# A diffusion layer on one core: splits off GpSimd, joined block transfers, keys over GpSimd's queue, unread products at the routing

## The chip, the core and the metric

The kernel runs on one of the eight cores of a Trainium2 chip. A core has five engines with queues of their own: TensorE (PE in the profile: matrix products into PSUM), VectorE (DVE), ScalarE (ACT), GpSimd (POOL) and SyncE (SP), which mostly issues DMA transfers; ScalarE and GpSimd issue some too. Each engine works through its instructions in order, and semaphores tie them together. The metric is device microseconds of one execution, the median of three runs.

## What is computed

One layer of a hybrid backbone over 1024 latent and 256 context tokens of width 1024: one input projection (2832 columns), softmax attention (8 query heads on 2 key heads of 64), a gated delta rule (4 heads of 128, both directions), one output projection, then 16 experts that each choose 128 tokens. The reference, cut:

```python
p_lat = h_lat @ w_in                      # split into aq ak av dq dk dv dz db da
...
att_lat = merge_heads(attend_blocked(q_l, k_all, v_all))   # softmax over context and latent keys
...
qkv = jax.nn.silu(short_conv(jnp.concatenate([dq, dk, dv], axis=-1), conv_w))
...
decay = jnp.exp(jnp.where(tril, g_cum[..., :, None] - g_cum[..., None, :], -jnp.inf))
a_strict = jnp.where(tril & ~eye, jnp.einsum('bhnid,bhnjd->bhnij', k_beta, k) * decay, 0.0)
unit_lower = a_strict + eye.astype(f32)
sol = lax.linalg.triangular_solve(unit_lower, rhs, left_side=True, lower=True, unit_diagonal=True)
...
def step(s, inp):                          # scan over chunks, once per direction
    v_new = u_c - jnp.einsum('bhck,bhkv->bhcv', w_c, s)
    s_next = s * gl_c[..., None, None] + jnp.einsum('bhck,bhcv->bhkv', kd_c, v_new)
    o = jnp.einsum('bhck,bhkv->bhcv', qd_c, s) + jnp.einsum('bhij,bhjv->bhiv', qk_c, v_new)
...
y_lat = jnp.concatenate([att_lat, dn_lat], axis=-1) @ w_out
x = x + g1 * y_lat
affinity = jax.nn.softmax((h @ router_w).astype(jnp.float32), axis=-1)
gates, idx = lax.top_k(jnp.swapaxes(affinity, 1, 2), cap)
hid = jax.nn.silu(xg @ w_gate) * (xg @ w_up)     # by expert
x = x + g2 * scatter_add((hid @ w_down) * gates)
```

## The kernel before, in words

The kernel is written in Python; a scheduler sets each engine's order of instructions at build time. Tokens go in 10 tiles of 128 (two of context, eight latent). float32 products are made from split operands, a high part (`whi`, `hh`, `ehi`) and a rest (`wlo`, `hl`, `elo`), three products for each.

**Stages** (us from the span's start): modulation and hidden tokens to 72; input projection to 411; attention groups with the scan steps of the delta rule to about 715; attention with the output projection and the routing to 978; experts to 1526; the last stores.

**Projection** (`in_proj`). The columns come in groups: keys and values of attention, then k, q, v of the delta rule (`conv_head`, `conv_tail`), attention queries (`queries`), the gate z (`out_gate`). `weights` loads each group's next weights (`wraw`), rounds them on ScalarE (`whi`, L425) and forms the rest `wlo` (L426), from the seventh group on GpSimd and earlier on VectorE. Between the groups `tick` draws steps from a generator (`prep`): the decay gates; `dn_chunk` for each of the ten chunks; the inverses (`dn_wave`); the rotary tables and the rotation of the attention keys (`sr_raw`, `sr_b`, `sr_sp`, stored in DRAM as `sks` and `sqs`).

`dn_chunk` loads k and q of one chunk, head-transposed (`kq`, L803 and L805, two transfers), and the cumulated decay spread over all partitions (`grow`, L807). GpSimd subtracts the token's own decay (L808), ScalarE makes Relu and exp of it (L814, L815: `Ef`, `Eb`, for latent chunks also `Eq`). TensorE multiplies k with k and q (L825, L827, into PSUM banks `ps_d`), VectorE multiplies the banks with the decays (L829, L830, L834), GpSimd masks (`affine_select`, L843), and SP stores `sN` and `sQ`. `kq`, `grow` and the decays have two buffers each.

`dn_wave` inverts the 32x32 diagonal blocks of 8 units at once (a unit is a chunk and a direction) by VectorE steps on `T` (L864, L866), in three waves; ScalarE makes a transposed copy (L869) and stores both in DRAM (`sT`, L870, L871). Wave 0 runs in the projection, the others beside the scans.

**Scans.** After `att_open` (which loads the rotated keys, `ksplit`, L1052, and transposes them, L1056) and `dn_open` (zeroed blocks `F` and `X`), each of ten rounds runs a `dn_step` in both directions and an attention group (`att_group`). A `dn_step` loads k, v, q, `kT` and the blocks of `sT` (`dn_merge`: eight transfers of 16 KB, L896, and `mN`, L898), merges the blocks to the inverse of 128x128 by small products (L907 to L942), and updates the state `S` (L975 to L1009). Attention goes by query blocks j (two tiles of tokens) and four head pairs hp: scores (L1112), transposes of the probabilities (L1122), values. `att_q(j)` prepares the block's transposed queries `QT` (L1080); it is called at hp = 2 of the block before, and for j = 0 at the first group.

**Routing.** Each expert's tokens are found by sorted lists that VectorE merges (`top_in`, `top_out`; L1402 spreads a list, L237 merges), then their minimum is spread (L1452), ranks are counted, the tokens of experts 0 and 1 picked (L1500) and gathered by GpSimd, and transposed (L1526). Then the experts' products begin (L1601).

The lines that the change moves, as they stand:

```python
(eng or nc.vector).tensor_tensor(lo[:, k:k + 4], raw, hi[:, k:k + 4], op=ALU.subtract)
...
nc.sync.dma_start(kq[:, :, 0], self.skT[c])
if lat:
    nc.sync.dma_start(kq[:, :, 1], self.sqT[c])
...
nc.gpsimd.tensor_tensor(gr, gr, self.gc[:, c, :, None].to_broadcast([P, 8, P]), op=ALU.subtract)
...
nc.sync.dma_start(s, self.sks[t0:t0 + T].rearrange("t p i d -> p t i d"))
...
if hp == 2 and j < 3:
    self.att_q(j + 1)
```

## Time and profile before

| | |
|---|---|
| median of 3 runs | 1551.98 us (1550.82 to 1552.12) |
| profiled execution | 1550.66 us |
| its span | 1548.9 us, mean granted clock 0.967 |
| PE busy | 1443.1 us (93%) |
| DVE busy | 1178.0 us (76%) |
| ACT busy | 949.0 us (61%) |
| POOL busy | 222.8 us (14%) |

Times in the rows count from the span's start. A busy PE row is not PE at its peak, since products overlap. A line of a view by stretches gives the stretch and its length, then the busy time with the number of instructions for PE, PEld (weight loads), DVE, ACT and POOL, then PE's granted clock (1.00 is full), the share of DMA and GB/s. A line of the waits names the engine and line that waited, the engine and line that it waited for, the total in us, the number of times and the longest. A line of the groups gives line, engine, operation, tiles, shapes and count, busy us and mean ns, then idle time before. In the timeline: start, duration, engine and line; in brackets the idle time before and what ended it. SPq is SP's DMA queue.

### The profile page before, as it was taken

How to read it: one execution, taken by the hardware profiler on the slowest of the kernel's cores; microseconds unless marked ns; L12 is line 12 of the kernel's file. 1: busy time of each engine (PE TensorE's matmuls, PEld its weight loads, DVE VectorE, ACT ScalarE, POOL GpSimd, SP SyncE). 2: the span in 40 equal slices, each digit the busy share in tenths (PEclk: the TensorE clock that was granted, in tenths of full speed). 3: DMA queues.
4: the chain of work that ended last, by engine and by line, in shares of the span. 5: the costliest groups of instructions: out<-in, count | busy, mean ns of one | idle time of the engine just before them, and what ended most of it. 6: DMA issues, size and time to landing. Idle time of an engine off the chain costs nothing.

```text
span 1548.9 us, 25613 instructions
## 1 busy us (share of the span) xinstructions
PE 1443.1 (93%) x9416; PEld 1173.8 (76%) x9416; DVE 1178.0 (76%) x2456; ACT 949.0 (61%) x1513; POOL 222.8 (14%) x230
## 2 busy tenths in 40 slices
PE   4899998997899999999899996799999999999997
PEld 1887787886777787788577664688888888888885
DVE  2825578698678686576574588899999999999996
ACT  2815455434285544566774543688888888888884
POOL 0000003423111121111400021111111111111101
PEclk7999999997999999999999998899999999999999
DMA  9356826777734456541342575889999999999992
GB/s 356 103 187 212 287 84 180 223 237 247 224 82 146 138 176 183 143 136 53 94 149 94 181 292 211 315 300 394 382 396 394 394 387 391 399 396 384 381 371 43
DMA packets 187048, 377.27 MB, mean 244 GB/s; under 512 B 47631, under 2 KB 124187, under 8 KB 159403
## 3 DMA queue, kind: packets, MB, share of 16 engines
q1 hardware_dynamic: 176320, 339.94, 61.9%
q0 software_dynamic: 7488, 29.36, 6.3%
q10 hardware_dynamic: 3115, 6.34, 1.1%
q8 instruction: 74, 1.21, 0.3%
q14 instruction: 51, 0.42, 0.1%
HBM read 321.91 MB, written 53.68 MB: 242 GB/s over the span
## 4 chain that ended last, share of the span: by engine, by line
PE 71%; DVE 12%; DMA 8%; ACT 5%; issue 2%; POOL 1%; SPq 1%; POOLq 0%; ACTq 0%; DVEq 0%
PE ps_m L1601 32%; PE ps_t L1129 4%; PE ps_a L1112 3%; PE ps_t L1122 3%; PE ps_s L441 3%; PE ps_s L443 3%; PE ps_s L442 3%; PE ps_t L1601 2%; PE ps_d L975 1%; DMA woraw<-in_w_out 1%; DMA sz<-zz 1%; PE ps_d L296 1%; PE ps_d L981 1%; PE ps_d L1284 1%; PE ps_d L1283 1%
## 5 line engine op out<-in xcount | busy, mean ns | idle before, releaser
L1601 PE MATMUL ps_m<-ehi,xx 128*128 128x512 f32 x1024 | 259.7, 396 | 0.4 <-DVE xx L1538 0.4
L1601 DVE TENSOR_TENSOR elo<-eraw,ehi 128x2048 fp32r<-128x2048 f32 x102 | 231.3, 2288 | 20.1 <-ACT ehi L1601 19.6
L1601 ACT ACTIVATE ehi<-eraw 128x2048 fp32r<-128x2048 f32 x105 | 201.3, 1918 | 54.7 <-PE ps_m L1601 45.4
L1601 PEld LDWEIGHTS ps_m<-ehi,xx 128*128 128x128 f32 x1024 | 189.9, 189 | 38.3 <-ACT xf L1534 0.8
L1601 PE MATMUL ps_m<-elo,xx 128*128 128x512 f32 x512 | 137.4, 390 | 0.0
L1601 PE MATMUL ps_m<-ehi,hx 128*128 128x512 f32 x512 | 129.7, 395 | 0.0
L1115 DVE TENSOR_SCALAR_CACHE_REDUCE prob<-ps_a 128x416 f32<-128x416 f32 (+1 forms) x192 | 109.4, 595 | 26.0 <-PE ps_a L1112 16.2
L1601 DVE TENSOR_TENSOR elo<-fraw,ehi 128x2048 fp32r<-128x2048 f32 x51 | 115.8, 2287 | 9.1 <-ACT ehi L1601 9.0
L1112 PE MATMUL ps_a<-kts,QT 128*128 128x416 f32 (+1 forms) x384 | 109.1, 390 | 4.0 <-DVE prob L1115 3.9
L1601 ACT ACTIVATE ehi<-fraw 128x2048 fp32r<-128x2048 f32 x51 | 97.8, 1917 | 24.2 <-PE ps_m L1601 21.4
L1601 PEld LDWEIGHTS ps_m<-elo,xx 128*128 128x128 f32 x512 | 96.3, 188 | 20.5
L1123 ACT ACTIVATE PT<-ps_t 128x512 f32<-128x512 f32 (+1 forms) x192 | 93.7, 525 | 28.8 <-PE ps_t L1122 26.9
L1601 PEld LDWEIGHTS ps_m<-ehi,hx 128*128 128x128 f32 x512 | 94.0, 188 | 18.2
L1122 PE MATMUL ps_t<-consts,prob 128*128 128x128 f32 x640 | 100.2, 282 | 3.1 <-ACT PT L1123 1.7
L433 PE MATMUL ps_s<-whi,hh 128*128 128x256 f32 (+1 forms) x336 | 98.0, 293 | 3.9 <-DVE zz L625 2.1
L1745 POOL DMA_INDIRECT out_x<-ey,idx x16 | 52.0, 3252 | 342.3 <-DVE ey L1601 342.3
L1118 ACT ACTIVATE prob<-prob,mn 128x1280 f32<-128x1280 f32 x64 | 87.2, 1363 | 19.1 <-DVE mn L1117 18.4
L435 PE MATMUL ps_s<-whi,hl 128*128 128x256 f32 (+1 forms) x336 | 95.8, 289 | 0.9 <-DVE hl L410 0.9
L434 PE MATMUL ps_s<-wlo,hh 128*128 128x256 f32 (+1 forms) x336 | 95.5, 287 | 0.0
L441 PE MATMUL ps_s<-hh,whi 128*128 128x512 f32 (+1 forms) x256 | 95.1, 372 | 0.0
L443 PE MATMUL ps_s<-hh,wlo 128*128 128x512 f32 (+1 forms) x256 | 94.3, 368 | 0.0
L442 PE MATMUL ps_s<-hl,whi 128*128 128x512 f32 (+1 forms) x256 | 94.0, 367 | 0.0
(434 smaller groups left out, 3134.5 us busy)
## 6 DMA issues: line engine op xcount, KB each, us to landing
eraw<-in_w_up SPq DMA_DIRECT2D x38, 1024.0 KB, 9.4
eraw<-in_w_down SPq DMA_DIRECT2D x32, 1024.0 KB, 7.0
eraw<-in_w_gate SPq DMA_DIRECT2D x31, 1024.0 KB, 8.8
wmod<-in_w_mod SPq DMA_DIRECT2D x24, 1024.0 KB, 6.3
fraw<-in_w_down SPq DMA_DIRECT2D x21, 1024.0 KB, 7.6
fraw<-in_w_gate SPq DMA_DIRECT2D x16, 1024.0 KB, 9.8
fqraw<-in_w_gate SPq DMA_DIRECT2D x16, 1024.0 KB, 9.7
fraw<-in_w_up SPq DMA_DIRECT2D x14, 1024.0 KB, 8.4
```

Source lines behind the costliest of these rows:

```text
L433: self.nc.tensor.matmul(ps[:, :n], self.hh[:, k, ts], hi[:, k, a:a + n], start=st, stop=False)
L434: self.nc.tensor.matmul(ps[:, :n], self.hh[:, k, ts], lo[:, k, a:a + n], start=False, stop=False)
L435: self.nc.tensor.matmul(ps[:, :n], self.hl[:, k, ts], hi[:, k, a:a + n], start=False, stop=en)
L441: self.nc.tensor.matmul(ps[:, :n], hi[:, k, a:a + P], self.hh[:, k, ts], start=st, stop=False)
L442: self.nc.tensor.matmul(ps[:, :n], hi[:, k, a:a + P], self.hl[:, k, ts], start=False, stop=False)
L443: self.nc.tensor.matmul(ps[:, :n], lo[:, k, a:a + P], self.hh[:, k, ts], start=False, stop=en)
L1112: nc.tensor.matmul(ps[:, k0:min(k0 + 512, w)], QT[:, h, i], self.KTs[:, kv * 2 + x, ks], start=x == 0, stop=x == 1)
L1115: v.tensor_scalar(pr[:, c0:c0 + w], ps[:, :w], -1.0, 3e38, op0=ALU.mult, op1=ALU.min, accum_out=mn[:, y:y + 1])
L1118: nc.scalar.activation(pr, pr, AF.Exp, bias=mn[:, 3:4], scale=-1.0, accum_out=rs[:, a, hp, i:i + 1])
L1122: nc.tensor.transpose(pt[:, x * P:(x + 1) * P], pr[:, (k0 + x) * P:(k0 + x + 1) * P], self.ident)
L1123: nc.scalar.activation(PT[g][:, :, a, i], pt[:, :n * P].rearrange("p (x q) -> p x q", x=n), AF.Copy)
L1601: i = fn(*args, **kw)
```

## The change

1. **Splits.** `wlo` is always formed on VectorE. The subtraction on `grow` goes; ScalarE's Relu takes the token's decay as a bias instead, one instruction for each head (`gc` or its negative `ngc`, made once).
2. **Joined transfers.** k and q lie side by side in DRAM (`skq`), so that `dn_chunk` and `dn_step` load both at once. The inverse blocks lie in `sT` with their transposes next to each other, and `F` and `X` are one tile `FX`: four transfers of 32 KB in a `dn_merge` for eight of 16 KB. The transposed copy is made by VectorE and the `sT` stores are issued by SP.
3. **Queues.** `ksplit` (with buffers of its own) and `sr_sp<-sqs` are loaded by GpSimd's queue. `att_q(0)` is called right after `att_open`, `att_q(j + 1)` at hp = 1.
4. **z and router.** `zz` has four buffers and tanh is taken in place; the router's loads and constants come earlier.
5. **Unread products.** `spin` issues products of 128x512 (bf16) whose result nobody reads: 18 behind the last list's products, 10 behind the picks.

```diff
-            (eng or nc.vector).tensor_tensor(lo[:, k:k + 4], raw, hi[:, k:k + 4], op=ALU.subtract)
+            nc.vector.tensor_tensor(lo[:, k:k + 4], raw, hi[:, k:k + 4], op=ALU.subtract)
...
-        self.skT = self.dr.tile([NT, P, DH, P], F32, name="skT")
-        self.sqT = self.dr.tile([NT, P, DH, P], F32, name="sqT")
+        self.skq = self.dr.tile([NT, P, DH, 2, P], F32, name="skq")
...
-                self.out_gate(hi, lo, h)
                 if h:
                     self.router_consts(self.wp)
+                self.out_gate(hi, lo, h)
...
-            th = self.wp.tile([P, 256], F32, name="zt", bufs=1)
-            nc.scalar.activation(th, ps[:, :256], AF.Tanh, scale=0.5)
-            z = self.wp.tile([P, 256], F32, name="zz", bufs=2)
-            nc.vector.scalar_tensor_tensor(z, th, 1.0, ps[:, :256], op0=ALU.add, op1=ALU.mult)
+            z = self.zp.tile([P, 256], F32, name="zz", bufs=4)
+            nc.scalar.activation(z, ps[:, :256], AF.Tanh, scale=0.5)
+            nc.vector.scalar_tensor_tensor(z, z, 1.0, ps[:, :256], op0=ALU.add, op1=ALU.mult)
...
-        nc.sync.dma_start(kq[:, :, 0], self.skT[c])
-        if lat:
-            nc.sync.dma_start(kq[:, :, 1], self.sqT[c])
+        nc.sync.dma_start(kq if lat else kq[:, :, 0], self.skq[c] if lat else self.skq[c, :, :, 0])
...
-        nc.gpsimd.tensor_tensor(gr, gr, self.gc[:, c, :, None].to_broadcast([P, 8, P]), op=ALU.subtract)
...
-            nc.scalar.activation(e, gr[:, 4 * d:4 * d + 4], AF.Relu, scale=sg)
+            off = self.ngc if sg > 0 else self.gc
+            for h in range(DH):
+                u = 4 * d + h
+                nc.scalar.activation(e[:, h], gr[:, u], AF.Relu, bias=off[:, c, u:u + 1], scale=sg)
...
-        nc.scalar.copy(Tt[:n], T[:n].rearrange("p i j -> p j i"))
-        nc.scalar.dma_start(sT[0, :n], T[:n].rearrange("p i j -> p (i j)"))
-        nc.scalar.dma_start(sT[1, :n], Tt[:n].rearrange("p i j -> p (i j)"))
+        nc.sync.dma_start(sT[:, 0].rearrange("g (b r) -> g b r", b=4), T[:n].rearrange("p i j -> p (i j)"))
+        v.tensor_copy(Tt[:n], T[:n].rearrange("p i j -> p j i"))
+        nc.sync.dma_start(sT[:, 1].rearrange("g (b r) -> g b r", b=4), Tt[:n].rearrange("p i j -> p (i j)"))
...
-            pr = slice(32 * b, 32 * b + 32)
-            cb = 32 * (b % 2)
-            for dst, o in ((F[pr, :, 32 * b:32 * b + 32], of), (X[pr, :, cb:cb + 32], ox)):
-                nc.sync.dma_start(dst, dram(sT, o * P * 1024 + base + b * 1024, [[32, 32], [4096, DH], [1, 32]]))
+
+            nc.sync.dma_start(FX[32 * b:32 * b + 32, :, 32 * b:32 * b + 32], dram(sT, base + b * 1024, [[32, 32], [4096, 2 * DH], [1, 32]]))
...
-            s = tp.tile([P, 2048], F32, name="ksplit", tag="PT4", bufs=2)[:, :512 * T]
+            s = (tw if T == 2 else tp).tile([P, 512 * T], F32, name="ksplit", tag=f"PT{T}", bufs=2)
...
-            nc.sync.dma_start(s, self.sks[t0:t0 + T].rearrange("t p i d -> p t i d"))
+            nc.gpsimd.dma_start(s, self.sks[t0:t0 + T].rearrange("t p i d -> p t i d"))
...
-            nc.sync.dma_start(s, self.sqs.rearrange("t p n d -> p t n d"))
+            nc.gpsimd.dma_start(s, self.sqs.rearrange("t p n d -> p t n d"))
...
-        if (j, hp) == (0, 0):
-            self.att_q(0)
-        if hp == 2 and j < 3:
+        if hp == 1 and j < 3:
             self.att_q(j + 1)
...
+            if t == NLAT - 1:
+                self.spin("d", 18, listed)
...
+    def spin(self, tag, n, behind):
+
+        ps = self.bank(tag)
+        with self.tc.issue_after(behind.ins):
+            for _ in range(n):
+                last = self.nc.tensor.matmul(ps, self.oneb, self.info.rearrange("p t e c -> p (t e c)")[:, :512], start=True, stop=True)
+        return last
...
+        self.spin("m", 10, self.picked)
```

What this does to the order of the instructions, at three places. A row gives the line, the operation, what is written from what, and the shape.

SP's queue in the attention queries' part of the projection, before: the loads of the second to fourth latent chunk's `kq` among the loads of keys to be rotated.

```order
L1027 DMA sr_raw<-skr 128x4x128
L636 DMA sq<-zz 128x256
L803 DMA kq<-skT 128x4x128
L636 DMA sq<-zz 128x256
L805 DMA kq<-sqT 128x4x128
L846 DMA sQ_1_3421<-Qb 128x512
...
L803 DMA kq<-skT 128x4x128
L805 DMA kq<-sqT 128x4x128
```

The same place on SP after the change (`sT` are the stores of the first wave's inverses, `sQ` a chunk's masked products).

```order
L807 DMA kq<-skq 128x1024
L1027 DMA sr_raw<-skr 128x4x128
L638 DMA sq<-zz 128x256
L809 DMA grow<-sgc 128x1024 x2
L807 DMA kq<-skq 128x1024
L638 DMA sq<-zz 128x256
L850 DMA sQ_1_3478<-Qb 128x512
L874 DMA sT_2788<-T 32x4x1024
L876 DMA sT_2788<-L 32x4x1024
...
L807 DMA kq<-skq 128x1024
L1027 DMA sr_raw<-skr 128x4x128
```

The third latent chunk's `kq` stood behind the third `sr_raw` load and now stands ahead of it, and the fourth chunk's too; the two `sT` stores are new here and stand ahead of the fourth.

TensorE around the transposes of the third query block (L1080) before the change; L935 to L1009 are scan steps, L1122 and L1112 attention. They stand in the fifteenth `dn_step` of TensorE's order.

```order
L935 MATMUL ps_d<-F_4193,mN_6959 64x64 x4
L975 MATMUL ps_d<-S_6612,kT_7010 128x128 x3
L940 MATMUL ps_d<-q_6993,X_4197 64x64 x4
L975 MATMUL ps_d<-S_6612,kT_7010 128x128
L981 MATMUL ps_d<-svv_7001,F_4193 128x128
L1080 MATMUL ps_t<-consts,sr_sp 128x128 x8
```

And after the change:

```order
L975 MATMUL ps_d<-S_5967,kqT_6308 128x128
L1110 MATMUL ps_a<-kts,QT 128x416 x2
L981 MATMUL ps_d<-svv_6301,F_4278 128x128 x4
L1080 MATMUL ps_t<-consts,sr_sp 128x128 x6
L990 MATMUL ps_d<-vn_6324,skk_6300 128x128 x4
L1003 MATMUL ps_d<-S_5967,kqT_6308 128x128 x4
L1080 MATMUL ps_t<-consts,sr_sp 128x128 x6
```

They moved to the twelfth `dn_step`, with scores (L1110) of the block before still beside them.

TensorE at the last list before the change (L1402 spreads it, L1452 takes the spread minimum), and after it.

```order
L1402 MATMUL ps_l<-srt_10838,consts 16x32 x4
L1452 MATMUL ps_m<-consts,m_10886 128x16
```

```order
L1405 MATMUL ps_l<-srt_10773,consts 16x32 x4
L1431 LDWEIGHTS oneb
L1431 MATMUL ps_d<-info,oneb 128x512
...
L1465 MATMUL ps_m<-consts,m_10840 128x16
```

The pair on L1431 stands there 18 times, between the list's products and the minimum's.

## Rows read from the trace of the kernel before

**Rows 1.** Busy time by stretches of the span, core 0.

```profile
240.00:280.00 40.00, 34.53 (x183) 29.04 (x182) 34.53 (x52) 20.28 (x36) 20.46 (x15) 0.96 0.80 233
280.00:320.00 40.00, 37.85 (x280) 35.85 (x280) 24.48 (x63) 15.88 (x31) 10.18 (x10) 0.96 0.74 214
320.00:360.00 40.00, 27.02 (x216) 25.73 (x214) 38.01 (x104) 15.83 (x26) 17.07 (x9) 0.84 0.72 230
360.00:400.00 40.00, 37.41 (x295) 36.44 (x296) 31.70 (x101) 15.96 (x30) 6.32 (x9) 0.94 0.74 236
400.00:440.00 40.00, 35.11 (x279) 31.54 (x277) 25.65 (x82) 21.94 (x45) 7.68 (x13) 0.91 0.75 203
620.00:640.00 20.00, 16.92 (x154) 15.02 (x153) 11.80 (x28) 10.32 (x22) 4.40 (x4) 0.83 0.52 155
955.00:980.00 25.00, 7.53 (x70) 6.36 (x71) 21.30 (x93) 7.67 (x10) 7.64 (x11) 0.50 0.76 300
1040.00:1080.00 40.00, 40.00 (x192) 33.21 (x191) 38.16 (x28) 32.35 (x28) 6.82 (x3) 1.00 1.01 395
```

**Rows 2.** Waits of TensorE, 240 to 425 us.

```profile
PE ps_d L825 <- issue: 12.4, 2, 11.2
PE ps_d L827 <- DVE Eb L834: 4.3, 1, 4.3
PE ps_d L825 <- DVE rs_a L130: 3.3, 1, 3.3
PE ps_a L1056 <- DVE rbias L1208: 2.7, 1, 2.7
...
PE ps_s L433 <- ACT zz L635: 1.8, 1, 1.8
```

**Rows 3.** Timeline, 350 to 357 us: SP's queue and TensorE.

```profile
351.29 0.37 SPq L1027 DMA_DIRECT2D sr_raw<-skr  x1
...
352.30 0.53 SPq L803 DMA_DIRECT2D kq<-skT  x1
...
356.15 1.19 PE L825 MATMUL ps_d<-kq 128*128 128x256 f32 x2 [11.18 <-issue]
```

**Rows 4.** Waits of SP's DMA queue, 235 to 440 us.

```profile
SPq L1027 <- DVE sr_b L495: 9.4, 1, 9.4
```

**Rows 5.** Groups by shape: POOL 235 to 440, DVE 235 to 411, L426 whole span.

```profile
L808 POOL TENSOR_TENSOR grow<-grow,g_gc 128x1024 f32<-128x1024 f32 x10 | 20.4, 2038 | 34.4 <-DMA grow<-sgc 34.4
L426 POOL TENSOR_TENSOR wlo<-wraw,whi 128x1024 fp32r<-128x1024 f32 x8 | 20.0, 2506 | 44.1 <-ACT whi L425 38.2 <-PE ps_t L690 6.0
...
L661 DVE SCALAR_TENSOR_TENSOR cacc<-craw,cw,cacc 128x1284 f32<-128x1284 f32 x12 | 22.1, 1841 | 0.4
...
L426 DVE TENSOR_TENSOR wlo<-wraw,whi 128x1024 fp32r<-128x1024 f32 x12 | 14.6, 1222 | 24.6 <-ACT whi L425 16.9 <-PE ps_t L690 7.7
```

**Rows 6.** Groups of ScalarE by shape: 235 to 411 us, and the whole span.

```profile
L814 ACT ACTIVATE Ef<-grow 128x512 f32<-128x512 f32 x10 | 6.3, 628 | 18.6 <-DVE rs_i L126 6.5 <-POOL grow L808 6.1 <-DMA sN<-Ef 3.1
...
L695 ACT ACTIVATE cjunk<-ps_t 128x128 bf16<-128x128 f32 x72 | 19.9, 276 | 1.5
```

**Rows 7.** DMA issues with count, size and us to landing.

```profile
h<-xn POOLq DMA_DIRECT2D x4, 512.0 KB, 5.9
...
ksplit<-sks SPq DMA_DIRECT2D x1, 512.0 KB, 4.8
```

**Rows 8.** Timeline of TensorE, 620 to 632 us.

```profile
630.36 1.97 PE L1080 MATMUL ps_t<-consts,sr_sp 128*128 128x128 f32 x8 [0.27 <-DVE sr_sp L500]
```

**Rows 9.** Timeline of TensorE, 955 to 1001 us.

```profile
965.54 0.61 PE L1452 MATMUL ps_m<-consts,m 16*128 16x16 f32 x2 [6.39 <-DVE m L237]
...
976.21 1.97 PE L1526 MATMUL ps_t<-consts,xg 128*128 128x128 f32 x8 [3.77 <-DMA xg<-h,idx]
978.62 3.75 PE L1601 MATMUL ps_m<-ehi,xx 128*128 128x512 f32 x8 [0.43 <-DVE xx L1538]
...
983.16 2.00 PE L1601 MATMUL ps_m<-ehi,xx 128*128 128x512 f32 x8
```

More of the change, by code (lines that the diff above doesn't have):

```diff
@@ L150, in build @@
         self.att_open()
+        self.att_q(0)
         self.dn_open()
@@ L559, in in_proj @@
             if i + 1 < len(groups):
-                W.append(self.weights(groups[i + 1][1], 256, eng=nc.gpsimd if i > 5 else nc.vector))
+                W.append(self.weights(groups[i + 1][1], 256))
             hi, lo = W.pop(0)
@@ L570, in in_proj @@
                 self.close("cp")
+                self.zp = self.open("zp")
+                self.router_loads(self.wp)
             if nm == "z" and h == 0:
@@ L595, in in_proj @@
         self.close("kp")
+        self.close("zp")
         self.close("pp")
@@ L680, in conv_tail @@
         if name != "v":
-            st = self.sqT if name == "q" else self.skT
+            st = self.skq[:, :, :, 1 if name == "q" else 0]
             for c0, n in parts:
@@ L757, in gates @@
         v.tensor_copy(tot.rearrange("p c u -> p (c u)"), ps[:, 80:160])
+        self.ngc = new("ngc", k)
+        v.tensor_scalar(self.ngc, self.gc, -1.0, None, op0=ALU.mult)
         self.egc, self.ekd, self.egl = new("egc", k), new("ekd", k), new("egl", k)
@@ L876, in dn_open @@
         sp = self.sp = self.open("sp")
-        self.F = [[sp.tile([P, DH, P], F32, name=f"F{d}{i}") for i in range(2)] for d in range(2)]
-        self.X = [[sp.tile([P, DH, 64], F32, name=f"X{d}{i}") for i in range(2)] for d in range(2)]
+        self.FX = [[sp.tile([P, 2 * DH, P], F32, name=f"F{d}{i}") for i in range(2)] for d in range(2)]
         for d in range(2):
             for i in range(2):
-                nc.gpsimd.memset(self.F[d][i], 0.0)
-                nc.gpsimd.memset(self.X[d][i], 0.0)
+                nc.gpsimd.memset(self.FX[d][i], 0.0)
         self.so = [[self.dr.tile([P, DH, P], F32, name=f"so{d}_{t}") for t in range(NLAT)] for d in range(2)]
@@ L1179, in out_weights, with router_loads @@
                 yield 1
-    def router_consts(self, pool):
-        nc, A, k = self.nc, self.A, self.keep
-        v = nc.vector
+    def router_loads(self, pool):
+        nc, A = self.nc, self.A
         m = pool.tile([P, 5, KT], F32, name="m2c")
@@ L1189, in router_consts @@
         nc.sync.dma_start(m[:, 4], self.col(A["norm2_w"], 0))
+        rw = pool.tile([P, KT, NE], F32, name="rw")
+        nc.sync.dma_start(rw, dram(A["router_w"], 0, [[KT * NE, P], [1, KT * NE]]).rearrange("p (k e) -> p k e", k=KT))
+        self.router = m, rw
+    def router_consts(self, pool):
+        nc, k = self.nc, self.keep
+        v = nc.vector
+        m, rw = self.router
         self.sh2 = k.tile([P, KT], F32, name="sh2")
@@ L1401, in top_out @@
                 for g in range(4):
-                    nc.tensor.matmul(ps[:, g], self.ident[:, 32 * g + NE:32 * g + 32], srt, start=True, stop=True)
+                    listed = nc.tensor.matmul(ps[:, g], self.ident[:, 32 * g + NE:32 * g + 32], srt, start=True, stop=True)
+            if t == NLAT - 1:
+                self.spin("d", 18, listed)
             L = self.os.tile([NE, 4, 32], F32, name="lists", bufs=2)
@@ L1499, in expert_pick @@
         for t in range(NLAT):
-            self.nc.tensor.matmul(ps[:, :5], oh[:, t], self.info[:, t, e], start=t == 0, stop=t == NLAT - 1)
+            self.picked = self.nc.tensor.matmul(ps[:, :5], oh[:, t], self.info[:, t, e], start=t == 0, stop=t == NLAT - 1)
         return ps
```

35 lines of the change are left out of this document (16 added, 19 removed).

## The prediction

> **What bounds the kernel now.** I read the busy time by stretches first, since the share over the whole span hides the stages [rows 1]. In the experts, from 1040 us on, TensorE has 40.00 us of work in 40.00, and the change touches nothing there. In the projection it has 34.53, 37.85, 27.02 and 37.41 us in four stretches of 40, late in the scans 16.92 of 20, around the routing 7.53 of 25. So the change can gain what lies in those holes and in the slow clock behind them, and no more.
>
> Next, TensorE's waits in the projection [rows 2]: five lines come to 12.4 + 4.3 + 3.3 + 2.7 + 1.8 = 24.5 us. The largest single one, 11.2 us, is put down to "issue", which names nobody; the timeline does [rows 3]. SP issues in order. Its load of `sr_raw` went out at 351.29, after 9.4 us of waiting for VectorE's `sr_b` [rows 4], and the chunk's `kq` load stood behind it and went at 352.30; the products that read it began at 356.15. The 4.3 us wait is VectorE being late with a chunk's `Eb`. Why it is late the groups by shape show [rows 5]: a convolution step on 128x1284 takes 1841 ns, where a weight split on VectorE, 128x1024, takes 1222, which would be 1532 at that length. GpSimd spends 20.4 us on the `grow` subtraction and 20.0 us on eight weight splits in just this time, and its split takes 2506 ns.
>
> The clock adds to it. A stretch's granted clock tells how long it was at the low level (1.2 GHz): (1 - clock) x 40, doubled. From 240 to 440 that is 3.2, 3.2, 12.8, 4.8 and 7.2 us, 31.2 in all. Some 14.5 of it (11.2 + 3.3) TensorE stood idle; the other 16.7 us of work ran at half speed and lost about 8. The projection's holes are thus worth 24.5 + 8, about 33 us.
>
> **The change part by part.** *GpSimd's splits.* Eight pieces move to VectorE at 1222 ns: 9.8 us more there. Against it goes the stretching of its other work. From below that is the one line shown, 12 x (1841 - 1532) = 3.7 us; from above half of GpSimd's 40.4 us, 20. I take 16, near the top, since VectorE was busy 34.53 and 38.01 us in the two stretches in which GpSimd worked most. The transposed copy of the inverse comes over from ScalarE: between 1.2 us (the split of the same size) and 2.5 (the same on GpSimd). `ngc` is below 0.3. VectorE's sum over 240 to 400 is 128.7 us; it becomes 128.7 - 16 + 9.8 + 2 + 0.3, about 125, in a stretch that I expect to last 140. That is 89% busy, and the reason why I don't take all 33 us.
>
> *The Relu by head.* 28 activations of 128x512 at 0.63 us become 112 of 128x128 [rows 6]. The nearest row of that shape is 276 ns, and one can't cost more than the 128x512 does: each of the 28 costs 4 x 0.28 - 0.63 = 0.5 us to 4 x 0.63 - 0.63 = 1.9 us more, 14 to 53 us over the projection; I take the near end. ScalarE has 68 us of work in those 160, so it fits beside TensorE. `Ef` and `Eb` come later by this much, but earlier by the 2 us of GpSimd's subtraction that they had waited for. I take zero; at the far end it is part of rival 1.
>
> *`kq` in one load, and its place.* In the order the `kq` loads of the second and third latent chunk now stand ahead of the third `sr_raw` load, so that load's 9.4 us no longer hold them. What is late next is a PSUM bank: a chunk's later products need VectorE to have emptied the chunk before, and that work now stands among the last inverse steps, with the transposed copy. I keep 4 of the 11.2 us, the other 1.2 of that line, and half of the 3.3. The 4.3 us on `Eb` go with the stretching. Four `zz` buffers end the 1.8 us (a buffer that waited for its store). The router constants, moved ahead, end the 2.7 us at 411, and with it the slow 7.2 us behind (3.6 lost). New small waits, as TensorE closes up to a busy VectorE, I put at 4 us and 1 of clock. Left over: 4 + 1.2 + 1.6 + 4 + 1, about 12 of 33. **Projection -21 us**; bounds -8 (only the waits on `Eb` and `rbias` end, 4.3 + 2.7 + 1) and -32.
>
> *Keys by GpSimd's queue.* The three `ksplit` loads and `sr_sp` stand behind the last mask selects, not among the `sz` stores. A 512 KB transfer on GpSimd's queue lands 5.9 us after its issue, `ksplit` on SP 4.8 [rows 7]: 1.1 us later each, but they can start earlier, having buffers of their own. The memsets of `FX` now stand behind them, ahead of the first scan steps, where TensorE has attention to do. I take 0, bounds -3 and +4. The Trainium skill has a rule against this edit ("SBUF — State Buffer", SBUF: two separate sides): GpSimd writes the descriptors of the transfers it issues, and a VectorE instruction that takes both ports locks it out meanwhile, 620 ns alone against 3100 ns beside such a copy. By it, as an estimate from that page, the four loads would come 2.5 us late each, 10 in all. The 5.9 against 4.8 us of the rows doesn't show so much, but the rows have no such load beside a full VectorE either; by rows it is rival 4.
>
> *Inverse blocks.* Eight loads of a scan step become four of twice the size, and `kT` and `q` one. That spares SP's issuing; I see no hole of TensorE that SP's issuing makes in the scans, so alone 0. The three waves' `sT` stores move from ScalarE's queue into SP's, which is rival 3.
>
> *Queries one group earlier.* From 620 to 640 TensorE idled 3.1 us, and the clock of 0.83 makes 6.8 us at the low level, 3.4 lost: 6.5 together. The transposes of the third query block, which free the next scores, ran only at 630.36 [rows 8]. In the order they now stand in the twelfth scan step instead of the fifteenth, so scores lie between the late scan products. **-4 us**, bounds 0 and -8 (the same hole a little before 620).
>
> *Unread products.* Before the lists' maximum TensorE idles 6.4 us; 18 products go there. At the low clock eight products took 3.75 us, later 2.00 [rows 9]: 0.44 and 0.23 each by their starts. If only the first eight are slow, as there, they last 3.5 + 10 x 0.23 = 5.8 us and fit; if all are, 8 us, and the maximum's product comes 1.5 us late. Ten more stand before the gather's transposes, 2.3 to 4.4 us in a gap of 3.8: up to 0.6 us late. The gain is the first experts' products at full clock, 1.75 us, and something of the same for the eight transposes (1.97 us now). **-2 us**, bounds +2 and -3.
>
> Sum: -21 + 0 + 0 - 4 - 2 = -27 us. The profiled execution took 1550.66 us, its span 1548.9 and 1.8 around it; the median of the runs is 1551.98, 1.3 above. From the median that is 1525.
>
> **The rivals.**
> (1) *VectorE takes the hole over.* If the stretching was only 5 us, VectorE's sum is about 136 us of 160, and the waits change their releaser more than their length: projection -8, scans -2, routing -1, so 1541. For it: 38.01 us busy of 40 at 320. Against: two thirds of GpSimd's work there goes.
> (2) *Everything closes up.* Projection -32, scans -8, routing -3: 1509. Against: 89% of an in-order engine.
> (3) *Slower: SP held by `sT`.* The stores of the inverses wait in SP's queue for VectorE's last inverse step and its copy; behind them stand a `kq` load and other stores, and in the scans the loads of the next steps. Three waves that hold SP as `sr_b` did, 9.4 us, are 28 us, with 1.6 of slow clock behind each (half of the 3.2 above) 33, all of it exposed and on top of a projection that gains nothing from `kq`: with the rest of my sum (-27 + 7) it comes to 1552 - 20 + 33 = 1565. It decides as soon as more than 20 of the 33 reach TensorE. Against: the order lets two `kq` loads out ahead, and the scans have attention beside them.
> (4) *The keys are held on GpSimd's queue.* If each of four issues is held by one VectorE instruction of the splits' size, 1.2 to 2.5 us, and lands 1.1 later, the transposes of the keys start up to 14 us later than I think: 1539. Against: 5.9 and 4.8 us are near each other.
> (5) *It cancels*: 1552, where the chunks' new order costs a stall as large as the one that ends.
>
> **How the numbers follow.** Forecast 1525 (1515 to 1534): 0.55. Rival 1: 0.17; rival 2: 0.14; rival 3: 0.06; rival 4: 0.04; rival 5: 0.04. The range takes in rivals 1 and 4 and stops at the edge of rival 2: 1510 to 1542. A measurement of this kernel tells about 0.2% (3 us) from no change. Faster 0.55 + 0.17 + 0.14 + 0.04 = 0.90, same 0.04, slower 0.06.
>
> **What would show it.** TensorE's first key transpose, at 411 us before, behind its wait for `rbias`, should start at 388 to 395. No wait on "issue" above 5 us in the chunks' products. GpSimd without `wlo` and `grow`, the convolution step near 1532 ns. TensorE above 38 us in each 40 of 580 to 660. Granted clock 1.0 at 980. It would be wrong with VectorE above 95% from 240 to 390 and waits on `Eb` or `zz` of the old sum (rival 1), with SP waiting over 9 us at an `sT` store while a load that TensorE needs stands behind (rival 3), or with the maximum's product over 1 us behind its merge.

## The result, and the profile after

The changed kernel takes 1535.43 us, median of four runs (1530.05 to 1542.01), against 1552.05 before: a ratio of 0.9886, 95% interval [0.9853, 0.9919], so 16.6 us or 1.1% less. The forecast was 1525 with a range of 1510 to 1542; sign and range held, though 1535.43 lies just outside the narrower 1515 to 1534 of the forecast itself, and the forecast gain of 27 us was 10 too large. The runs of the changed kernel lie 12 us apart, and the traces show a part of why (below); the kernel before, run 25 times in a later round, spread over 13 us (1546.14 to 1559.39). The profiled execution is the slowest of the four: 1542.0 us, span 1540.3.

Busy time by stretches of the changed kernel, the same columns as [rows 1]: stretch, length, busy time of PE, PEld, DVE, ACT, POOL, PE's granted clock, DMA share, GB/s.

```profile
240.00:280.00 40.00, 37.53 (x209) 31.73 (x209) 32.74 (x62) 30.93 (x80) 4.41 (x9) 1.00 0.82 251
280.00:320.00 40.00, 39.14 (x314) 38.09 (x313) 28.30 (x70) 18.01 (x44) 3.37 (x4) 1.00 0.75 224
320.00:360.00 40.00, 38.24 (x296) 37.09 (x295) 38.20 (x137) 25.36 (x66) 3.24 (x5) 1.00 0.90 297
360.00:400.00 40.00, 31.95 (x232) 31.33 (x231) 28.85 (x91) 12.27 (x29) 8.74 (x11) 0.88 0.70 233
400.00:440.00 40.00, 36.80 (x312) 29.94 (x311) 27.81 (x85) 27.36 (x53) 8.23 (x8) 0.91 0.54 135
520.00:560.00 40.00, 39.97 (x417) 33.05 (x417) 32.78 (x102) 17.84 (x40) 6.66 (x6) 0.91 0.61 177
620.00:640.00 20.00, 19.85 (x217) 16.10 (x214) 8.64 (x30) 9.45 (x23) 2.08 (x2) 1.00 0.50 142
```

The holes of [rows 1] up to 360 us are gone, 27.02 us of TensorE in the worst stretch have become 38.24, and the clock is 1.00 there. VectorE has as much to do as before (38.20 of 40), GpSimd a fifth. The hole between projection and attention, which stood at 400 to 440 before, now lies across 360 to 440. From 520 to 560 the clock is 0.91 although TensorE is busy 39.97 of 40 us.

TensorE's waits from 235 to 425 us, against [rows 2]:

```profile
PE ps_a L1056 <- DMA ksplit<-sks: 4.8, 1, 4.8
PE ps_s L434 <- DVE zz L627: 3.3, 1, 3.3
PE ps_t L1080 <- DMA sr_sp<-sqs: 1.4, 1, 1.4
...
PE ps_d L829 <- issue: 0.9, 1, 0.9
```

Nothing of the old five lines is left but 0.9 us on "issue". What ends last now is the load of the rotated keys. The groups by shape tell the rest, against [rows 5] and [rows 6]: the convolution step on VectorE, the split beside it, and Relu by head on ScalarE.

```profile
L663 DVE SCALAR_TENSOR_TENSOR cacc<-craw,cw,cacc 128x1284 f32<-128x1284 f32 x12 | 18.6, 1551 | 0.3
...
L427 DVE TENSOR_TENSOR wlo<-wraw,whi 128x1024 fp32r<-128x1024 f32 x8 | 9.7, 1220 | 0.7 <-PE ps_t L692 0.7
...
L818 ACT ACTIVATE Eb<-grow,g_gc 128x128 f32<-128x128 f32 x40 | 13.5, 389 | 0.0
```

1841 ns have become 1551 in the mean (1532 were forecast), the eight splits cost VectorE 9.7 us, and Relu on 128x128 takes 389 ns, not the 276 of the nearest row, without TensorE waiting for it.

**Where the time went, by stages.** The stages are cut at events of TensorE in each timeline: the projection's last product, the last scan product, the last list product, the first of the experts' products and the last of theirs with a high part (`ehi`). All in us; the lower rows are experiments.

| kernel | projection ends at | to the last scan | to the last list | to the experts | experts |
|---|---|---|---|---|---|
| before | 408.4 | 308.3 | 242.4 | 19.5 | 559.0 |
| changed, first trace | 394.1 | 307.1 | 250.9 | 19.4 | 557.3 |
| changed, second trace (again) | 392.2 | 313.4 | 250.4 | 18.9 | 557.3 |
| nospin | 392.3 | 307.2 | 245.0 | 19.1 | 558.2 |
| keys_sp | 394.9 | 317.3 | 250.7 | 19.4 | 557.3 |
| early_keys | 391.5 | 323.2 | 247.4 | 19.0 | 557.3 |
| keys_apart | 393.7 | 310.0 | 241.6 | 19.2 | 557.3 |
| late_q | 391.4 | 307.2 | 244.5 | 19.3 | 557.2 |
| q_mixed | 390.8 | 306.9 | 249.6 | 19.3 | 557.3 |
| zz_router | 392.2 | 307.1 | 246.2 | 18.7 | 557.3 |
| pool_grow | 395.1 | 310.9 | 246.8 | 18.3 | 557.3 |
| pool_wlo | 405.2 | 309.0 | 251.2 | 19.2 | 557.3 |
| poolsplit | 409.4 | 305.9 | 250.3 | 19.1 | 557.3 |
| only_splits | 400.9 | 315.0 | 245.8 | 19.0 | 558.9 |

For the first trace: -14.3 in the projection, -1.2 to the last scan product, +8.5 in attention's tail and the output projection, -0.1, and -1.7 in the experts: -8.8 us, where the spans differ by 8.6. The last stage but two, which no edit was meant to touch, gave back more than half of what the projection won.

### The profile page after: what moved, and what is told of

Its sections match the earlier page's. It is cut to its first block, busy times and chain, and to the rows that moved or that the text cites. A ratio compares the mean times of both kernels' runs of the same rounds, so it can differ in the third digit from the quotient of the medians.

```text
span 1540.3 us, 25579 instructions
## 1 busy us (share of the span) xinstructions
PE 1459.0 (95%) x9442; PEld 1187.9 (77%) x9444; DVE 1168.5 (76%) x2468; ACT 959.0 (62%) x1594; POOL 186.7 (12%) x212
## 4 chain that ended last, share of the span: by engine, by line
PE 75%; DVE 8%; DMA 5%; ACT 5%; issue 2%; SPq 1%; POOL 0%; POOLq 0%; DVEq 0%; ACTq 0%
PE ps_m L1614 32%; PE ps_a L1110 4%; PE ps_t L1120 4%; PE ps_t L1127 4%; PE ps_s L442 3%; PE ps_s L444 3%; PE ps_s L443 3%; PE ps_t L1614 2%; PE ps_d L975 2%; PE ps_d L1287 2%; PE ps_d L1285 1%; PE ps_d L1286 1%; PE ps_d L981 1%; PE ps_d L990 1%; PE ps_d L297 1%
## 5 line engine op out<-in xcount | busy, mean ns | idle before, releaser
L1110 PE MATMUL ps_a<-kts,QT 128*128 128x416 f32 (+1 forms) x384 | 113.1, 401 | 5.3 <-DVE prob L1113 5.3
L1116 ACT ACTIVATE prob<-prob,mn 128x1280 f32<-128x1280 f32 x64 | 87.3, 1364 | 16.9 <-DVE mn L1115 16.4
```

Source lines behind the costliest of these rows:

```text
L1110: nc.tensor.matmul(ps[:, k0:min(k0 + 512, w)], QT[:, h, i], self.KTs[:, kv * 2 + x, ks], start=x == 0, stop=x == 1)
L1116: nc.scalar.activation(pr, pr, AF.Exp, bias=mn[:, 3:4], scale=-1.0, accum_out=rs[:, a, hp, i:i + 1])
```

## The experiments

### The changed kernel once more: again

No edit.

> The changed kernel once more, unchanged. Its four runs so far lie 12 us apart (1530 to 1542), those before it 1.3. Theory: the same stalls, of about the same length, now and then cost a stretch of low TensorE clock (6.9 us at half speed) and now and then don't; then this trace and the first one agree in the stalls within 1 us each and differ in the places where the granted clock is 0.5, and the times again spread over 1530 to 1542. Rival: a transfer whose landing varies (keys over GpSimd's queue, 7 to 12 us in the first trace); then the wait for ksplit (4.8 us) differs between the two.

Measured: 1541.76 us (1535.16 to 1545.07), 0.9909 [0.9876, 0.9942]. The wait for `ksplit` was 9.9 us here, against 4.8 in the first trace: the loads went out 1.1 us later and the first landed after 9.2 us, not 7.2. So the rival has a part: one transfer's landing differs between executions. The clock fell at other places too, and once where TensorE had no idle time, in both traces of the changed kernel. Busy time of again (first fence) and of nospin (second), whose TensorE order is the same up to the routing:

```profile
530.00:535.00 5.00, 5.00 (x58) 4.15 (x54) 4.50 (x12) 2.53 (x6) 1.05 (x1) 0.62 0.65 200
535.00:540.00 5.00, 5.00 (x25) 4.60 (x25) 2.58 (x9) 1.80 (x5) 1.08 (x1) 0.50 0.40 118
```

```profile
530.00:535.00 5.00, 5.00 (x57) 4.40 (x47) 4.68 (x15) 4.31 (x10) 0.07 (x1) 1.00 0.54 142
```

Just before, TensorE had run 16-row products (a group of 32, 1.96 us) and the 32x32 products of the block merge. The same stretch went on at full clock in one execution and at half in two.

### The unread products: nospin

```diff
-            if t == NLAT - 1:
-                self.spin("d", 18, listed)
...
-        self.spin("m", 10, self.picked)
```

> The changed kernel without the 28 unread products. Theory: they are worth 1.5 to 2 us, because the experts begin at full clock: without them the first eight products of the experts take 3.75 us again instead of 2.0, and the time is 1.5 to 2 us longer. Rival 1: they delay the lists' minimum and the picks; then it is 0.5 to 1.5 us shorter. Rival 2: they keep the clock up for nothing, 0.

Measured: 1539.06 us, 0.9918 [0.9892, 0.9945], not to be told from again. The traces are sharper. TensorE's timeline of the changed kernel, and of nospin:

```profile
952.90 5.69 PE L1431 MATMUL ps_d<-info,oneb 128*128 128x512 bf16 x16 [0.22 <-issue]
958.64 0.39 PE L1465 MATMUL ps_m<-consts,m 16*128 16x16 f32 x2
...
965.26 4.05 PE L1431 MATMUL ps_m<-info,oneb 128*128 128x512 bf16 x9 [0.24 <-issue]
969.10 1.83 PE L1539 MATMUL ps_t<-consts,xg 128*128 128x128 f32 x8
971.45 2.09 PE L1614 MATMUL ps_m<-ehi,xx 128*128 128x512 f32 x8 [0.51 <-DVE xx L1551]
```

```profile
950.44 0.61 PE L1463 MATMUL ps_m<-consts,m 16*128 16x16 f32 x2 [5.97 <-DVE m L238]
...
961.19 1.97 PE L1537 MATMUL ps_t<-consts,xg 128*128 128x128 f32 x8 [3.85 <-DMA xg<-h,idx]
963.59 3.05 PE L1612 MATMUL ps_m<-ehi,xx 128*128 128x512 f32 x8 [0.43 <-DVE xx L1549]
```

With the products the experts' first eight take 2.09 us, without 3.05; the experts' stage is 0.9 us shorter (557.3 against 558.2) and the way to it as long (19.4 and 18.9 against 19.1). The ten before the transposes ran at the low clock (4.05 us), and the transposes followed without a wait. Worth about 1 us, less than these runs can tell.

### GpSimd's splits, all back: poolsplit

```diff
+                W.append(self.weights(groups[i + 1][1], 256, eng=nc.gpsimd if i > 5 else nc.vector))
...
+        nc.gpsimd.tensor_tensor(gr, gr, self.gc[:, c, :, None].to_broadcast([P, 8, P]), op=ALU.subtract)
...
+            nc.scalar.activation(e, gr[:, 4 * d:4 * d + 4], AF.Relu, scale=sg)
```

> The changed kernel with the eight weight splits and the subtraction on grow back on GpSimd and Relu in whole instructions, all else as changed. Theory: most of the projection's gain is VectorE freed from stretching; then the convolution step goes from 1551 back to about 1841 ns, the first key transpose comes 8 to 12 us later (407 to 411 instead of 399) and the time is 8 to 12 us longer. Rival: the gain comes from the kq loads standing ahead of the sr_raw load and from the zz buffers; then the first key transpose moves by less than 4 us.

Measured: 1553.77 us, 1.0002 [0.9983, 1.0021]: with this one part undone nothing is left of the gain. The convolution step is back at 1819 ns, the projection ends at 409.4, and TensorE waits as before:

```profile
PE ps_d L825 <- issue: 12.2, 1, 12.2
PE ps_a L1052 <- DMA ksplit<-sks: 8.6, 1, 8.6
PE ps_d L827 <- DVE Eb L834: 4.4, 1, 4.4
```

Here `kq` stands ahead in SP's order, and still the wait on "issue" is 12.2 us. The timeline of SP, GpSimd, VectorE and TensorE there, of poolsplit:

```profile
334.18 0.56 SPq L805 DMA_DIRECT2D kq<-skq  x1
...
347.43 2.35 POOL L427 TENSOR_TENSOR wlo<-wraw,whi 128x1024 fp32r<-128x1024 f32 x1 [12.40 <-ACT whi L426]
...
348.06 1.79 DVE L867 TENSOR_TENSOR T<-T,Ttmp 128x60 f32<-128x60 f32 x1
...
349.85 1.90 POOL L808 TENSOR_TENSOR grow<-grow,g_gc 128x1024 f32<-128x1024 f32 x1
...
350.18 1.61 DVE L865 TENSOR_TENSOR Ttmp<-L,T 128x31 f32<-128x31 f32 x1
351.70 2.35 POOL L427 TENSOR_TENSOR wlo<-wraw,whi 128x1024 fp32r<-128x1024 f32 x1
351.71 2.37 DVE L125 TENSOR_SCALAR rs_i<-sr_s 128x8 int32<-128x8 int32 x1
...
354.01 1.89 POOL L808 TENSOR_TENSOR grow<-grow,g_gc 128x1024 f32<-128x1024 f32 x1
354.06 1.89 DVE L867 TENSOR_TENSOR T<-T,Ttmp 128x31 f32<-128x31 f32 x1
...
357.89 0.34 DVE L834 SCALAR_TENSOR_TENSOR Eb<-ps_d,g_bp,Eb 128x128 f32<-128x128 f32 x1
...
358.33 2.05 PE L825 MATMUL ps_d<-kq 128*128 128x256 f32 x4 [12.24 <-issue]
```

Counted off in order, ten `kq` loads and the products of ten chunks, the products at 358.33 are the eighth chunk's. Its `kq` went out at 334.18, 24 us ahead. They write a PSUM bank that VectorE still had to empty of the chunk before, and VectorE's last read of it ended at 358.23, 0.1 us ahead of them. So the product waited for VectorE, not for SP. And VectorE was late because of GpSimd: four of its small steps took 1.79, 1.61, 2.37 and 1.89 us, each ending within 0.1 us of the GpSimd instruction beside it. In the changed kernel the same four take 0.21, 0.34, 0.16 and 0.38 us. That is 6.6 of the 12.2 us.

### One part alone: only_splits

The edit of poolsplit the other way round, on the kernel before.

> The kernel before with one part of the change alone: the eight weight splits and the subtraction on grow leave GpSimd (VectorE, and Relu by head with a bias). Theory: this part alone ends the stretching of VectorE, so the convolution step takes about 1550 ns, the projection's last product comes 10 to 15 us sooner than before's 408 and the time is 10 to 15 us shorter. Rival: it needs the kq loads and the zz buffers beside it, since TensorE would wait for kq at the same place (11.2 us before): then less than 5 us.

Measured: 1550.86 us, 0.9982 [0.9963, 1.0001], not clear of no change. The convolution step falls to 1551 ns and the projection ends at 400.9, 7.5 us sooner, but a wait of 5.1 us on "issue" stays, at the eighth chunk's products again:

```profile
331.82 0.53 SPq L805 DMA_DIRECT2D kq<-skT  x1
...
349.48 0.35 DVE L838 SCALAR_TENSOR_TENSOR Eb<-ps_d,g_bp,Eb 128x128 f32<-128x128 f32 x1
...
349.93 2.05 PE L829 MATMUL ps_d<-kq 128*128 128x256 f32 x4 [5.09 <-issue]
```

Their `kq` had gone out 17 us ahead, and VectorE's last read of the bank ended 0.1 us ahead: here too it is VectorE, whose reads stand behind steps on the rotated keys. The scheduler also puts two scan steps ahead of all attention (the first scores at 440.5), and the way to the last scan product is 6.7 us longer. So the parts belong together: the projection ends at 408.4 with neither, at 409.4 with all but the splits, at 400.9 with the splits alone, and at 394.1 with both. Which of the other edits is worth the 6.8 us between the last two, no run tells apart; the `zz` buffers and the early router constants it is not, since without them the projection ends at 392.2 (zz_router, below).

### The two splits apart: pool_wlo and pool_grow

pool_wlo has the first line of poolsplit's edit, pool_grow the other two.

> The changed kernel with the eight weight splits back on GpSimd, the subtraction on grow still gone. Theory: the splits do half of the stretching (20.0 of 40.4 us of GpSimd's work), so about 7 us longer than the changed kernel, with VectorE's inverse steps and rotary steps stretched, the convolution less. Rival: it is the wait for wlo itself (2.5 us a piece against 1.2) or the grow subtraction in the chain of the decays, then 0 or all of the 13 to 16 us.

> The changed kernel with the subtraction on grow back on GpSimd (and Relu in whole instructions), the weight splits still on VectorE. Theory: the subtractions stretch the convolution (1551 ns goes to about 1750) and hold the decays, so the projection's last product comes 4 to 8 us later than in the changed kernel (392 to 394) and the time is as much longer. Rival: the weight splits were the whole of it (with them back on GpSimd the last product came at 405): within 2 us.

Measured: pool_wlo 1556.33 us, 1.0024 [1.0012, 1.0035]; pool_grow 1543.23 us, 0.9929 [0.9907, 0.995]. The weight splits are the larger part: with them back the projection ends at 405.2 and the convolution step takes 2026 ns; the subtraction alone costs the projection 1 to 3 us (395.1, convolution step 1806 ns). TensorE waits for `wlo` nowhere in pool_wlo's projection, so that rival falls. In pool_grow the convolution step is stretched nearly as much as before the change (1806 against 1841 ns), and still the projection ends within 3 us of the changed kernel's: the mean of this step, which the prediction took as its sign, does not set the time. It matters which step is stretched, and who waits behind it. pool_wlo also waits 11.1 us for the scan's first blocks (`F<-sT`), which the order put ahead of the keys.

### The queue of the keys: keys_sp

```diff
-            nc.gpsimd.dma_start(s, self.sks[t0:t0 + T].rearrange("t p i d -> p t i d"))
+            nc.sync.dma_start(s, self.sks[t0:t0 + T].rearrange("t p i d -> p t i d"))
...
-            nc.gpsimd.dma_start(s, self.sqs.rearrange("t p n d -> p t n d"))
+            nc.sync.dma_start(s, self.sqs.rearrange("t p n d -> p t n d"))
```

> The changed kernel with the three ksplit loads and sr_sp back on SP's queue. Theory: these loads on GpSimd's queue (0.8 us of issuing each, 7 to 12 us to landing) make the 4.8 us wait for ksplit, the 1.4 us for sr_sp and the low clock behind; then the first key transpose comes 4 to 5 us sooner after the projection's last product, and the time is 5 to 8 us shorter. Rival: their buffers lie in memory that the projection holds until its last stores, so that the queue does not matter: within 2 us, and the wait stays above 3 us.

Measured: 1545.06 us, 0.9947 [0.9924, 0.997], slower than the changed kernel by 6 to 9 us, so the theory falls on the time. On the spot it was nearly right: from the projection's last product to the keys' transposes 3.1 us instead of 4.8 to 10. But the scheduler, which counts SP's queue, laid the scan steps differently in TensorE's order: some 170 scan products with no attention between them, 25 us from 568 on, where the changed kernel has some 70 in 8 us. From the projection's end to the last scan product it took 317.3 us against 307.1 and 313.4.

### The keys' memory: early_keys and keys_apart

The first load of `ksplit` waits for several transfers and engines. GpSimd's timeline of the changed kernel:

```profile
391.66 1.80 POOL L1052 DMA_DIRECT2D ksplit<-sks  x2 [21.25 <-DMA sz<-zz]
394.40 0.72 POOL L1052 DMA_DIRECT2D ksplit<-sks  x1 [0.94 <-PE ps_s L436]
395.11 0.73 POOL L1070 DMA_DIRECT2D sr_sp<-sqs  x1
```

The tiles have their own names, but their memory is that of the projection's last tiles: the load went out when a `zz` store had landed, 20 us after the rotated keys were in DRAM (the last store at 367.5, landing 4.2 us later). early_keys puts the `ksplit` tiles where the chunks' tiles lay; keys_apart moves the `zz` pool instead.

```diff
+        ks = self.open("ks", side="right")
...
+            s = ks.tile([P, 512 * T], F32, name=f"ksplit{t0}")
```

```diff
-                self.zp = self.open("zp")
+                self.zp = self.open("zp", side="right")
...
-        if hp == 1 and j < 3:
+        if hp == 2 and j < 3:
```

> The changed kernel with the ksplit tiles in a pool of their own where the chunks' tiles lie, so that the loads no longer wait for the memory of the zz tiles. Theory: the loads go out at about 380 instead of 392, TensorE goes from the projection's last product to the keys' transposes with less than 2 us between (4.8 to 10 now), and the clock stays up there: 5 to 10 us shorter than the changed kernel. Rival: the loads are held on GpSimd's queue by something else (the masks, VectorE's port), or the next thing is as late (sr_sp, the scan's first loads): then less than 2 us.

> The kernel with att_q(j + 1) at hp = 2, and one more line: the pool of the zz tiles on the other side of SBUF, so that the ksplit tiles no longer lie where the last gate tiles are stored from. Theory: the wait for the zz stores is what holds the ksplit loads at 391 to 393; without it they go out by 388, TensorE waits less than 4 us for the keys (5 to 10 in the changed kernel), and the time is 3 to 6 us under that of the kernel with hp = 2 alone (1537, 0.9884 of before). Rival: the tiles now lie on others that are as late (rotated keys and queries, stored until 386 and after), or the landing of the loads on GpSimd's queue (7 to 12 us) is the limit: the wait stays above 4 us and the time within 2 us.

Measured: early_keys 1556.85 us, 1.0016 [1.0, 1.0032]. Its loads went out from 374.13 us on:

```profile
374.13 2.50 POOL L608 DMA_DIRECT2D ksplit<-sks  x3 [5.19 <-DVE rbias L1217]
```

TensorE went from the projection to the keys with no gap (391.5 and 391.3): the cause of the wait is shown. And it is 17 to 20 us slower than the changed kernel. The loss lies where the order that came of it has four scan steps in a row, 430 to 479 us, with no attention beside them. Busy time there, of early_keys:

```profile
440.00:480.00 40.00, 29.15 (x204) 24.67 (x205) 26.24 (x82) 8.15 (x20) 5.79 (x6) 0.50 0.44 130
```

In the changed kernel TensorE has 39.61 of these 40 us, at full clock. keys_apart: 1534.69 us, 0.9887 [0.986, 0.9913]. Its theory falls: the tiles now lie on others as late, the loads went out from 395 on, and TensorE waited 9.5 us for `sr_sp` and 4.5 for `ksplit`. Yet to the last scan product it took 310.0 us, no more than the changed kernel's 307.1 and 313.4: a longer hand-over need not show in the time.

### The queries: late_q and q_mixed

late_q undoes both query edits; q_mixed puts back hp = 2 alone.

```diff
-        self.att_q(0)
...
-        if hp == 1 and j < 3:
+        if (j, hp) == (0, 0):
+            self.att_q(0)
+        if hp == 2 and j < 3:
```

> The changed kernel with att_q(0) at the first group and att_q(j + 1) at hp = 2 again. Theory: the queries one group earlier keep scores beside the late scan steps; without it TensorE waits for ScalarE and VectorE by some 3 us around the fifteenth scan step and the clock falls there, so 4 to 6 us longer. Rival: the joined transfers have made the scan chain short enough; then within 2 us.

> The changed kernel with one line back: att_q(j + 1) at hp = 2, while att_q(0) stays early. Theory: what a scan stage costs goes by the longest stretch of scan products in TensorE's order with no attention between (2.4 us of such products in the changed kernel at the eleventh step, 6.5 with the keys on SP, 10.3 with the keys early, none with both query edits undone), because in such a stretch each product waits for ScalarE or VectorE and the clock falls. Here the order has none over 2 us: from the projection's last product to the last scan product 303 us or less (307 to 313 in the changed kernel), no low clock from 500 to 700, and the time 3 to 8 us under the changed kernel's. Rival: the clock falls there by chance and the order does not matter: as the changed kernel, within 2 us.

Measured: late_q 1534.21 us, 0.989 [0.9859, 0.9921]; q_mixed 1537.35 us, 0.9884 [0.9859, 0.9909]. Both are the changed kernel within the measurement, and from the projection's end to the last scan product they take 307.2 and 306.9 us against 307.1 and 313.4. The early queries are worth nothing that shows. The stretch of scan products without attention goes with the large losses (early_keys 323.2, keys_sp 317.3) but not with differences below 3 us: q_mixed has none and is no faster, and the clock fell at 528.8 there as well.

### zz and the router's constants: zz_router

```diff
-            z = self.zp.tile([P, 256], F32, name="zz", bufs=4)
+            z = self.zp.tile([P, 256], F32, name="zz", bufs=2)
...
-                if h:
-                    self.router_consts(self.wp)
                 self.out_gate(hi, lo, h)
+                if h:
+                    self.router_consts(self.wp)
```

> The changed kernel with two zz buffers for four and the router constants behind the last gate group again. Theory: the four buffers and the early constants are worth 1.8 + 2.7 us of waits; without them TensorE waits for zz and rbias again, the key transposes start 3 to 6 us later, and the time is 2 to 6 us longer. Rival: the wait for ksplit behind covers it, since the loads wait for the zz stores in both: within 2 us at the key transposes.

Measured: 1540.49 us, 0.9914 [0.989, 0.9939]. The rival holds: the projection ends at 392.2 all the same, the key transposes start at 402.6 (398.9 and 402.1 in the changed kernel), and TensorE waits 9.5 us for the router's constants where it had waited for `ksplit`. Two waits lie over one another there; ending one shows the other.

## Why the prediction was right, and where it was off

*Projection, -21 us.* 6.3 of it (2.7 for `rbias`, 3.6 of slow clock) lie behind the last product; for the projection itself 14.7 were forecast, and 14.3 and 16.2 came. The stretching of VectorE was the right cause, with 1551 ns for the step against 1532 forecast, and undoing it undid everything. From 235 us to the projection's last product VectorE's busy time fell from 138.9 to 131.5 us, with the splits and the copy in it; about 4 us less was forecast (128.7 to 125, counted to 400). The wait on `Eb`, the `zz` store and the bank ended; one new wait of 3.3 us on `zz`, with a low clock from 370 to 377, is the small change that was allowed for.

For the largest wait, 11.2 us, the reason given was wrong, and that its term came out near is luck. The wait was put to SP's queue, because a `kq` load went out at 352.30 and the products began at 356.15. But `kq` has two buffers and its loads run ahead: the ones that stand above as the second to fourth latent chunk's are the eighth to tenth of ten. The products at 356.15 are the eighth chunk's, and the load at 352.30 is the ninth's. Two rows of the kernel before:

```profile
333.79 0.53 SPq L803 DMA_DIRECT2D kq<-skT  x1
...
355.71 0.34 DVE L834 SCALAR_TENSOR_TENSOR Eb<-ps_d,g_bp,Eb 128x128 f32<-128x128 f32 x1
```

The eighth `kq` was under way 22 us before its products, and VectorE's last read of their bank ended 0.1 us before them. The bank, which the prediction had as what is late next, was what they waited for; moving `kq` in SP's order could not shorten this wait, and in poolsplit it did not.

*Keys by GpSimd's queue, 0, and `rbias`, -6.3.* This is the step that failed. "They can start earlier, having buffers of their own" was read from the diff; early_keys shows that those buffers lie on memory that the projection still held. So the load stayed tied to the last gate stores while the projection came 14 us forward, and a wait for `ksplit` of 4.8, 9.9 and 10.0 us (three traces) took the place of `rbias`, with the clock low behind it as before. From the projection's last product to the first score: 13.6 us before, 15.1, 20.6 and 20.0 after. Rival 4 had the place and the size (1539) but not the mechanism: the issues were held by memory, and landed 7.2 to 12.2 us after in the first trace, against the 5.9 of [rows 7]. VectorE had little to do in these microseconds, from 395 on. In early_keys the three `ksplit` loads went out beside a VectorE that was busy 2.53 of 2.70 us, and landed 6.6 to 9.3 us after, against 7.2 to 9.3, so what VectorE did there held nothing up. The Trainium skill has VectorE holding up the descriptors of such loads ("SBUF — State Buffer", SBUF: two separate sides) while it runs an instruction that takes both ports; whether one of that kind would have, no run here tells.

*Scans, -4.* The hole at 620 closed, 19.85 of 20 us against 16.92. But from the projection's end to the last scan product nothing was gained (307.1 to 313.4 against 308.3). TensorE stood idle 11.5 us of this stage before, and 10.9, 16.4 and 15.8 in the changed kernel, again and nospin: the hand-over took the place of the hole, and falls of the clock, at 530 and 571 in the first trace, came on top. late_q, with 19.80 of 20 us at 620, shows that the early queries were not what closed the hole.

*Unread products, -2.* About -1: 0.9 to 1.7 us at the experts, 0 on the way there.

*Signs and rivals 1 to 3.* Of the signs named, the first key transpose did not come as said: it started at 398.9 and 402.1, not at 388 to 395. The others did: 0.9 us on "issue", the convolution step at 1551 ns, TensorE 39.91 and 39.79 of 40 us from 580 to 660, the clock 1.00 from 975 to 985. VectorE did not become the bound; SP's longest wait at an `sT` store in the projection was 1.1 us. Not everything closed up, either.

*What was not in the sum.* From the last scan to the last list product nothing was changed, and it took 8.5 and 8.0 us longer in two traces and 2.6 in a third of the same order. Busy time of that stage before, changed, nospin and keys_apart:

```profile
716.70:959.10 242.40, 222.44 (x1470) 166.65 (x1468) 164.46 (x777) 142.52 (x308) 45.23 (x67) 0.98 0.45 154
```

```profile
701.20:952.10 250.90, 228.45 (x1467) 172.47 (x1466) 168.79 (x798) 140.97 (x307) 43.98 (x67) 0.94 0.43 149
```

```profile
699.50:944.50 245.00, 223.11 (x1465) 168.18 (x1464) 170.09 (x796) 140.63 (x307) 43.60 (x67) 0.97 0.44 153
```

```profile
703.70:945.30 241.60, 220.98 (x1471) 165.68 (x1470) 165.49 (x777) 142.58 (x308) 44.47 (x67) 0.99 0.45 155
```

By the working of the prediction the clock gives the time at the low level: (1 - 0.98) x 242.4 x 2 = 9.7 us, then 30.1, 14.7 and 4.8. Half of that taken off leaves 237.6, 235.9, 237.7 and 239.2 us. The stage is the same in all four; what differs is how long TensorE ran at 1.2 GHz. In all fourteen traces this working gives 236 to 240 us, for a stage that took 241.6 to 251.2.

So the 10 us between forecast and result lie in two places. From the projection's last product to the last scan product 10.3 us less were forecast (6.3 and 4), and -1.2, +5.1 and -1.1 came in the changed kernel, again and nospin. And the stage behind, where the clock decides, took 8.5, 8.0 and 2.6 us more, which were not in the sum. In the changed kernel's trace the falls stand at stalls of 1.3 to 2.6 us, on `prob`, `OT`, `rr` and the lists' `aff` and `t6x`; in the kernel before, stalls of 1.72 us on `prob` and 1.39 on `aff` passed without one. Whether the changed kernel falls there more often than before stays open, with one trace of the kernel before. No version beat the changed kernel beyond its interval.

## What to carry to other kernels

A load that goes out just ahead of a waiting product need not be the one that the product reads: where a tile has two buffers, count loads and products off against each other, and look for what ended last before the product (here VectorE's last read of the bank, 0.1 us ahead in three traces). A load can't start before the memory of its tile is free, whatever queue it is on: look at what its issue waited for, not at the tile's name. When an engine's order comes from a scheduler, moving one transfer can reorder a stage 100 us away, so look at the order of the whole program for stretches where a dependent chain stands alone.
